# Rotary halves rearranged inside SBUF, and one buffer for each set of queries, in a two-block transformer kernel

## The chip, the cores and the metric

One core of a Trainium2 chip runs the whole program in one launch. The metric is the device time of one execution in microseconds (us), the median over several. The engines are TensorE (PE, with its weight loads PEld), VectorE (DVE), ScalarE (ACT), GpSimd (POOL) and SyncE (SP). SP and POOL also issue DMA transfers, each on a queue of its own; all transfers run on the same 16 DMA engines.

## The reference

512 tokens of 1024 features pass two blocks. Block 1 has a bidirectional chunked retention with 8 heads of 64 query/key features, a Fourier branch and a feed-forward with a convolution. Block 2 has gated spatial mixing, windowed attention with 16 query heads and 4 key heads of 64 features, and a feed-forward of 16 experts, each of which takes the 64 tokens that fit it best. All of it is in float32. What matters here is that queries and keys are turned by position before they are used:

```
def rope_2d(t, row, col):
    ...
    half = RET_QK_DIM // 2
    t1, t2 = t[..., :half], t[..., half:]
    return jnp.concatenate([t1 * cos - t2 * sin, t1 * sin + t2 * cos], axis=-1).astype(t.dtype)

q = rope_2d(split_heads(q, RET_HEADS), row, col) * q_scale
k = rope_2d(split_heads(k, RET_HEADS), row, col)
...
s_loc = jnp.einsum('bqkrd,bskd->bkrqs', qn, kn, preferred_element_type=jnp.float32) * scale
```

## The kernel before, in words

Activations lie transposed, with features on the 128 partitions and the 512 tokens along the row. A dense layer (`dense_T`, L226) computes 128 output features at a time, a chunk: 8 steps over the 1024 input features, and at each step three products (`mm3`, L221), because every float32 operand is split into a high and a low part that TensorE multiplies at full rate. So a chunk is 24 products with 512 columns. `dense_tok` (L241) is the same with tokens on the output's partitions. The weights come by SP (`w_dma_to`, L98), are split by ScalarE and VectorE (`w_split_to`, L113) three tiles ahead, and are used in the order of one list. Every engine works through its instructions in the order in which the program writes them; where one waits, all behind it on that engine wait.

The weights' columns are sorted so that one chunk holds the first rotary halves of four heads (32 features each) and the next chunk their second halves. VectorE turns them: `rope_pair` (L790) in block 1 and `rope_pair2` (L1228) in block 2 take the two chunks t1, t2 from PSUM and write a tile `rr` with two parts, r1 and r2. In it partition 32 h + i holds feature i of head h. The score products need both halves of a head one under the other on 64 partitions. That rearrangement is the subject. Before, `packer` (L393) does it by way of DRAM: two stores on POOL, one for each half, and fetches on POOL that read the tile back in the other order:

```
d = dram.tile([4, 2, 32, n], dt, name=name)
...
eng.dma_start(d[:, b], src[:, b])
...
eng.dma_start(dst, d.rearrange("h b p t -> (b p) h t"))
```

Where both partition halves need the same data, the fetch is done twice (to partitions 0 to 63 and 64 to 127). The places are:
- block 1, two batches of four heads (loop over `bt`, L805): queries into `qd`, keys into `kd`, then the projection of the values (`dense_tok("v", ...)`, L879), then `scores` (L831), which begins with transposes of `kd` (L837).
- the context's keys of block 2 (`epi_ck`, L1106): `kct` into `kcd`, split at L1140.
- the keys of block 2 (`epi_k2`, L1275): into `kdd`, split into `kH`, `kL` at L1430.
- the queries of block 2 (`epi_q2`, L1255), four sets of four heads, each two chunks: ScalarE and VectorE split `rr` into `rh` and `rl` (`split`, L107), which are stored by four transfers. The high part is fetched to partitions 0 to 63 and the low part to 64 to 127 of `qS`, which has two buffers: sets 0 and 1 at once (`q_fetch`, L1249), sets 2 and 3 in the fourth unit of the attention (L1452), when the first two are no longer read. `rr`, `rh` and `rl` have one buffer each.

After the queries follow two half chunks of a gate (`gb_half`, L1299) and the values `v2`, then eight units of attention (`unit`, L1317): per head four products into two banks of PSUM (L1334 to L1337), two operations of VectorE into `pt` (L1338, L1341) and an exponential on ScalarE. At the end of the program come the experts: 384 tiles of weights of 1 MB each, issued on SP (`x_dma_to`, L1487), the first while the attention's output is projected.

Of the kernel before, what the change touches and what calls it, by code (L numbers as in the profile page):

```python
# [42 lines left out]
def block_kernel(ctx: ExitStack, tc: tile.TileContext, A, out):  # L43
# [106 lines left out]
    def ring(stay=None):  # L150
        """a pair of buffers for activations, RINGB in turn; four of them outlive the dense layers."""
        if stay is None:
            stay = turns[0] % RINGB >= RINGB - 4
            turns[0] += 1
        pool, n = (rpool, 4) if stay else (wpool, RINGB - 4)
        return tuple(pool.tile([128, L], F32R, name=t, tag=t, bufs=n) for t in ("aH", "aL"))

# [68 lines left out]
    def dense_T(keys, acts, epi, n=L, kc=KD, first=2, pre=None):  # L226
        """out^T chunk j = W_j^T h^T, weights stationary; the first chunks share the pass over k."""
# [13 lines left out]
    def dense_tok(key, g, acts, ntok, cols, ntiles, epi, mid=None):  # L241
        """out[token, cols] = h W, activations stationary."""
# [19 lines left out]
    # modulation vectors that are needed later: products and sums along rows of the transposed  # L262
    # weights on VectorE, a part with every tile of weights
# [59 lines left out]
    def rsqrt_(v, nt, tagp):  # L323
        """v -> 1/sqrt(v), with one Newton step."""
# [20 lines left out]
    def bcast(r, nt, p):  # L345
        """[token] per partition -> [128, tokens], the same on every partition."""
# [22 lines left out]
    def modnorm(src, pB, a, b, dst, n=L, ks=range(KD)):  # L369
        """dst[k] = split of (src(k) * rstd) * a(k) + b(k); two chunks in flight."""  # L370
# [22 lines left out]
    def packer(name, n, dt=F32):  # L393
        """rotary halves of four heads [(head, 32), half, n] -> [(half, 32), head, n] by way of DRAM."""
        d = dram.tile([4, 2, 32, n], dt, name=name)

        def store(eng, src):
            for b in range(2):
                eng.dma_start(d[:, b], src[:, b])

        def fetch(eng, dst):
            eng.dma_start(dst, d.rearrange("h b p t -> (b p) h t"))
        return store, fetch

    # =====================================================================
    # block 1
    # =====================================================================
# [37 lines left out]
    def pair_mm(kp):  # L445
        """shift and scale of two chunks of features: the partial sums."""
# [29 lines left out]
    def warm(n):  # L476
        """products nobody reads, to keep the clock of TensorE up."""
# [12 lines left out]
    def first_split(j, h, l):  # L490
        """the first weights; the context's buffers hold two of them until its norm."""
        split(h, l, raws.pop(j))
        sched["ns"] += 1
        sched["nu"] += 1
        ws[j] = (h, l)
# [40 lines left out]
    def ctx_norm(cx, cH, cL, a, b):  # L536
        """the three parts of the norm of a context, to be spread over other work."""
# [37 lines left out]
    # the first projections run along with the arrival of the modulation  # L575
# [95 lines left out]
    # context of block 1: the two retention states  # L671
    # decays: lg = -exp(a), and the decay weights of the context tokens
# [8 lines left out]
    # decays of a chunk: its last state, the states' updates by token, queries to states, keys to queries  # L681
# [21 lines left out]
    # fourier mixing  # L703
# [79 lines left out]
    # retention, two batches of four heads  # L783
# [3 lines left out]

    packs = [packer(f"pk{i}", L) for i in range(4)]
# [16 lines left out]
    for bt in range(2):  # L805
# [3 lines left out]
        def epi_qk(j, ps, qd=qd, kd=kd):  # L809
# [7 lines left out]
            def emit(rr):  # L817
                store, fetch = packs.pop()
                store(nc.gpsimd, rr)
                fetch(nc.gpsimd, dst[0:64])  # L820
                fetch(nc.gpsimd, dst[64:128])
# [9 lines left out]
        def scores(h4, qd=qd, kd=kd, bt=bt):  # L831
            """within chunks: scores of keys (on partitions) and queries; keys by token for the states."""
# [20 lines left out]
        def states(h4, ke, bt=bt):  # L853
            """the states that each chunk meets: forward on partitions 0-63, backward on 64-127."""
# [39 lines left out]
        for h4 in range(4):  # L894
            ke, P, qs = nxt
            # gate projection of the head
# [52 lines left out]
    # the gates of the retention branch, while the last heads are normalized  # L949
# [9 lines left out]
    def merge_stage(key, acts, d_g, d_m, pool, tag, bufs, free, bias=None, hook=None):  # L959
        """ring chunks of d_m + d_g * (W^T acts), both operands from DRAM."""  # L960
# [49 lines left out]
    # feed-forward with the depthwise convolution  # L1010
# [86 lines left out]
    # =====================================================================  # L1097
    # block 2
    # =====================================================================
    # k, v of the context  # L1100
# [5 lines left out]
    def epi_ck(j, ps):  # L1106
        nc.scalar.activation(kct[:, j], ps, AF.Copy)
        if j == 1:
            store, fetch = packer("pkc", 256)
            store(nc.gpsimd, kct)  # L1110
            fetch(nc.gpsimd, kcd[0:64])
            fetch(nc.gpsimd, kcd[64:128])
    dense_T([("ck2", j) for j in range(2)], chl, epi_ck, n=256)

    # final norm of block 1 and first norm of block 2 from two sums
# [31 lines left out]
    # gated spatial mixing  # L1147
# [9 lines left out]
    def spatial_bias():  # L1157
        """the sums of the spatial weights times the shift join the spatial bias."""
# [56 lines left out]
    # window attention  # L1215
# [12 lines left out]
    def rope_pair2(t1, t2, emit):  # L1228
        ab = rq.tile([128, 2, L], F32, name="ab2", tag="ab2", bufs=1)
        rr = rq.tile([128, 2, L], F32, name="rr", tag="rr", bufs=1)  # L1230
# [16 lines left out]
    qfetch = {}  # L1247

    def q_fetch(kv):  # L1249
        q = ap.tile([128, 4, L], F32R, name="qS", tag="qS", bufs=2)  # L1250
        for i, fetch in enumerate(qfetch.pop(kv)):
# [809 lines left out]
```

## Time and profile before

| what | us |
|---|---|
| median of 3 runs | 2402.28 (2400.93 to 2404.88) |
| span of the profiled execution | 2399.6 |
| PE busy | 2252.9 (94%) |
| DVE, ACT, POOL busy | 1062.8, 658.2, 148.0 |
| chain that ended last, by engine | PE 62%, DMA 32%, ACT 2%, DVE 2% |

The span runs from the first to the last instruction of one profiled execution. That execution's own device time isn't listed apart; the median of the runs is 2.7 us above the span. The profile has several views: the chain of waits (what released what, from the last instruction back), tables of busy time by stretches of the span, rows of each engine in order of time with the idle time before each and what ended it, and the DMA issues with the time from issue to landing. [...]

### The profile page before, as it was taken

How to read it: one execution, taken by the hardware profiler on the slowest of the kernel's cores; microseconds unless marked ns; L12 is line 12 of the kernel's file. 1: busy time of each engine (PE TensorE's matmuls, PEld its weight loads, DVE VectorE, ACT ScalarE, POOL GpSimd, SP SyncE). 2: the span in 40 equal slices, each digit the busy share in tenths (PEclk: the TensorE clock that was granted, in tenths of full speed). 3: DMA queues.
4: the chain of work that ended last, by engine and by line, in shares of the span. 5: the costliest groups of instructions: out<-in, count | busy, mean ns of one | idle time of the engine just before them, and what ended most of it. 6: DMA issues, size and time to landing. Idle time of an engine off the chain costs nothing.

```text
span 2399.6 us, 28202 instructions
## 1 busy us (share of the span) xinstructions
PE 2252.9 (94%) x11052; PEld 1452.8 (61%) x11052; DVE 1062.8 (44%) x2059; ACT 658.2 (27%) x1033; POOL 148.0 (6%) x248
## 2 busy tenths in 40 slices
PE   9998999999999999998899999999898989898987
PEld 6887878878888887887776784434232323232322
DVE  4644666679787865435467552112111111111112
ACT  5532234344243544321366431000000000000002
POOL 0211000100112110001111000000000000000000
PEclk9999999999999999999899999999999999999999
DMA  8646254734456553246521488999999999999996
GB/s 311 237 169 193 82 157 156 258 117 153 157 186 212 159 153 106 88 128 157 148 67 27 153 322 349 410 420 420 420 421 420 420 421 420 420 421 420 420 421 277
DMA packets 138869, 623.68 MB, mean 260 GB/s; under 512 B 23600, under 2 KB 28336, under 8 KB 89712
## 3 DMA queue, kind: packets, MB, share of 16 engines
q1 hardware_dynamic: 109200, 557.59, 60.0%
q0 software_dynamic: 29536, 64.28, 9.8%
q8 instruction: 87, 1.43, 0.2%
q14 instruction: 46, 0.38, 0.0%
HBM read 600.01 MB, written 21.76 MB: 259 GB/s over the span
## 4 chain that ended last, share of the span: by engine, by line
PE 62%; DMA 32%; ACT 2%; DVE 2%; issue 1%; POOL 0%; SPq 0%; DVEq 0%; POOLq 0%; ACTq 0%
DMA xw<-in_w_exp_dram 27%; PE mm L222 12%; PE mm L224 12%; PE mm L223 12%; PE pgu L1760 5%; PE py L1818 3%; DMA pk<-rr 2%; DMA pq<-rl 2%; PE sm L1383 1%; PE mm L1371 1%; PE b L255 1%; PE b L253 1%; PE b L254 1%; PE b L222 1%; PE ps L1693 1%
## 5 line engine op out<-in xcount | busy, mean ns | idle before, releaser
L1760 PE MATMUL pgu<-xw,xt 128*64 128x512 f32 x2032 | 481.1, 602 | 56.8 <-DMA xw<-in_w_exp_dram 52.6
L222 PE MATMUL mm<-aH,wh 128*128 128x512 f32 (+1 forms) x1104 | 422.8, 383 | 6.7 <-DVE ab L1234 3.4
L224 PE MATMUL mm<-aH,wl 128*128 128x512 f32 (+1 forms) x1104 | 420.3, 381 | 3.8 <-DVE wl L131 3.8
L223 PE MATMUL mm<-aL,wh 128*128 128x512 f32 (+1 forms) x1104 | 420.0, 380 | 0.0
L1760 PEld LDWEIGHTS pgu<-xw,xt 128*64 128x64 f32 x2032 | 131.3, 136 | 355.3 <-issue 196.8
L131 DVE TENSOR_TENSOR wl<-wraw,wh 128x1024 fp32r<-128x1024 f32 (+1 forms) x212 | 256.2, 1213 | 172.2 <-ACT wh L122 171.8
L122 ACT ACTIVATE wh<-wraw 128x1024 fp32r<-128x1024 f32 (+1 forms) x212 | 220.0, 1044 | 253.2 <-PE mm L223 182.7
L222 PEld LDWEIGHTS mm<-aH,wh 128*128 128x128 f32 x1104 | 210.2, 190 | 46.7 <-issue 2.9
L224 PEld LDWEIGHTS mm<-aH,wl 128*128 128x128 f32 x1104 | 210.0, 190 | 43.6 <-DVE wl L131 4.8
L1818 PE MATMUL py<-xw,hTe 128*64 128x512 f32 x944 | 215.0, 598 | 19.4 <-DMA xw<-in_w_exp_dram 19.3
L223 PEld LDWEIGHTS mm<-aL,wh 128*128 128x128 f32 x1104 | 210.0, 190 | 38.0 <-DVE aL L383 0.4
L1818 PEld LDWEIGHTS py<-xw,hTe 128*64 128x64 f32 x944 | 64.9, 136 | 158.0 <-issue 111.4
L1788 DVE TENSOR_TENSOR eg<-pgu,eg 128x512 f32<-128x512 f32 x32 | 22.1, 692 | 253.8 <-PE pgu L1760 244.6
L1831 DVE SCALAR_TENSOR_TENSOR y<-py,sw,g2B 128x512 f32<-128x512 f32 x15 | 11.3, 751 | 221.1 <-PE py L1818 221.1
L1750 ACT ACTIVATE hTe<-pT 128x512 f32<-128x512 f32 x32 | 19.1, 597 | 313.6 <-PE pT L1749 313.6
L1726 DVE TENSOR_TENSOR aH<-ps,aH 128x512 f32<-128x512 f32 x56 | 38.8, 692 | 123.2 <-PE ps L1723 123.2
L108 ACT ACTIVATE yh<-y 128x512 fp32r<-128x512 f32 x17 | 10.7, 630 | 254.7 <-DVE y L1831 239.8
L282 POOL DMA_DIRECT2D mraw<-in_w_adaT_dram x96 | 51.5, 537 | 304.1 <-DVE mod L297 298.4
L1873 POOL TENSOR_TENSOR aH<-aH,fg 128x512 f32<-128x512 f32 x4 | 5.0, 1279 | 1037.1 <-ACT sqf L1872 1037.1
L222 PE MATMUL mm<-gH,wh 128*128 128x512 f32 x176 | 68.6, 390 | 0.0
L224 PE MATMUL mm<-gH,wl 128*128 128x512 f32 x176 | 68.6, 390 | 0.0
L223 PE MATMUL mm<-gL,wh 128*128 128x512 f32 x176 | 68.5, 389 | 0.0
(488 smaller groups left out, 3108.1 us busy)
## 6 DMA issues: line engine op xcount, KB each, us to landing
xw<-in_w_exp_dram SPq DMA_DIRECT2D x379, 1024.0 KB, 19.9
mraw<-in_w_adaT_dram POOLq DMA_DIRECT2D x96, 256.0 KB, 2.9
wraw<-in_w_up_dram SPq DMA_DIRECT2D x44, 512.0 KB, 3.8
wraw<-in_w_kv_tok_dram SPq DMA_DIRECT2D x20, 512.0 KB, 4.3
wraw<-in_w_bg_dram SPq DMA_DIRECT2D x16, 512.0 KB, 3.7
mraw<-in_w_modT_dram POOLq DMA_DIRECT2D x32, 256.0 KB, 4.6
mraw<-in_w_modT_dram SPq DMA_DIRECT2D x32, 256.0 KB, 4.2
wraw<-in_w_out_dram SPq DMA_DIRECT2D x16, 512.0 KB, 4.9
```

Of the source, the lines that this page charges most:

```text
L122: nc.scalar.activation(h[:, :sz], r[:, :sz], AF.Copy)
L131: nc.vector.tensor_tensor(*lows.pop(0), OP.subtract)
L222: nc.tensor.matmul(ps, wh, xh, start=first, stop=False)
L223: nc.tensor.matmul(ps, wh, xl, start=False, stop=False)
L224: nc.tensor.matmul(ps, wl, xh, start=False, stop=last)
L253: nc.tensor.matmul(ps[t][:, :cols], xh[:, ts], wh[:, s], start=k == 0, stop=False)
L254: nc.tensor.matmul(ps[t][:, :cols], xl[:, ts], wh[:, s], start=False, stop=False)
L255: nc.tensor.matmul(ps[t][:, :cols], xh[:, ts], wl[:, s], start=False, stop=k == KD - 1)
L282: eng.dma_start(t, A["w_modT" if b == 1 else "w_adaT"][c, hf])
L1726: nc.vector.tensor_tensor(x, p, x if e else xtok[:, t, c], OP.add)
L1760: nc.tensor.matmul(pgu[w][64 * i:64 * i + 64, :], xt[:, kq, es], t[2 * k + i], start=kq == 0, stop=kq == 7, skip_group_check=True)
L1818: nc.tensor.matmul(py[64 * hf:64 * hf + 64, :], lhs, t[2 * i + hf], start=f8 == 0 and i == 0, stop=f8 == 7 and i == 1, skip_group_check=True)
```

## The change

`packer` goes, and so do its tiles in DRAM. `pack` moves each of the eight pieces of 32 partitions (head h, half b) from its place in SBUF to its new place with a transfer of its own on POOL; `pack_twice` then copies partitions 0 to 63 to 64 to 127 with one more. The queries of block 2 are packed at once into four buffers of `qS`, and the late fetches fall away. `rr`, `rh` and `rl` of block 2 have two buffers. The reserve in SBUF for POOL's DMA descriptors is set to 2048 bytes of each partition. Comments and doc strings are taken out, which moves line numbers; they aren't shown here.

```
-    def packer(name, n, dt=F32):
-        d = dram.tile([4, 2, 32, n], dt, name=name)
-
-        def store(eng, src):
+    def pack(eng, dst, src, base=0):
+        for h in range(4):
             for b in range(2):
-                eng.dma_start(d[:, b], src[:, b])
-
-        def fetch(eng, dst):
-            eng.dma_start(dst, d.rearrange("h b p t -> (b p) h t"))
-        return store, fetch
+                eng.dma_start(dst[base + 32 * b:base + 32 * b + 32, h], src[32 * h:32 * h + 32, b])
+
+    def pack_twice(eng, dst, src):
+        pack(eng, dst, src)
+        eng.dma_start(dst[64:128], dst[0:64])
...
-    packs = [packer(f"pk{i}", L) for i in range(4)]
...
             def emit(rr):
-                store, fetch = packs.pop()
-                store(nc.gpsimd, rr)
-                fetch(nc.gpsimd, dst[0:64])
-                fetch(nc.gpsimd, dst[64:128])
+                pack_twice(nc.gpsimd, dst, rr)
...
-            store, fetch = packer("pkc", 256)
-            store(nc.gpsimd, kct)
-            fetch(nc.gpsimd, kcd[0:64])
-            fetch(nc.gpsimd, kcd[64:128])
+            pack_twice(nc.gpsimd, kcd, kct)
...
-        rr = rq.tile([128, 2, L], F32, name="rr", tag="rr", bufs=1)
+        rr = rq.tile([128, 2, L], F32, name="rr", tag="rr", bufs=2)
...
-    qfetch = {}
-
-    def q_fetch(kv):
-        q = ap.tile([128, 4, L], F32R, name="qS", tag="qS", bufs=2)
-        for i, fetch in enumerate(qfetch.pop(kv)):
-            fetch(nc.gpsimd, q[i * 64:i * 64 + 64])
-        qS[kv] = q
...
             def emit(rr):
-                rh = rq.tile([128, 2, L], F32R, name="rh", tag="rh", bufs=1)
-                rl = rq.tile([128, 2, L], F32R, name="rl", tag="rl", bufs=1)
+                rh = rq.tile([128, 2, L], F32R, name="rh", tag="rh", bufs=2)
+                rl = rq.tile([128, 2, L], F32R, name="rl", tag="rl", bufs=2)
                 split(rh, rl, rr)
-                qfetch[kv] = []
-                for i, s in enumerate((rh, rl)):
-                    store, fetch = packer(f"pq{kv}{i}", L, F32R)
-                    store(nc.gpsimd, s)
-                    qfetch[kv].append(fetch)
-                if kv < 2:
-                    q_fetch(kv)
+                qS[kv] = ap.tile([128, 4, L], F32R, name="qS", tag="qS", bufs=4)
+                pack(nc.gpsimd, qS[kv], rh)
+                pack(nc.gpsimd, qS[kv], rl, 64)
...
-            store, fetch = packer("pk2", L)
-            store(nc.gpsimd, rr)
-            fetch(nc.gpsimd, kdd[0:64])
-            fetch(nc.gpsimd, kdd[64:128])
+            pack_twice(nc.gpsimd, kdd, rr)
...
-            if u == 3 and ia in (3, 7):
-                q_fetch(2 + ia // 4)
...
-    nc = _bacc.Bacc("TRN2", target_bir_lowering=False, num_devices=1)
+    nc = _bacc.Bacc("TRN2", target_bir_lowering=False, num_devices=1, dynamic_dma_scratch_size=2048)
```

The instructions on POOL in block 1, both batches, before (`pk` are the tiles in DRAM):

```order
L399 DMA pk_1520<-rr 4x32x512 x2
L402 DMA qd<-pk_1520 64x4x512 x2
L399 DMA pk_1519<-rr 4x32x512 x2
L402 DMA kd<-pk_1519 64x4x512 x2
L399 DMA pk_1518<-rr 4x32x512 x2
L402 DMA qd<-pk_1518 64x4x512 x2
L399 DMA pk_1517<-rr 4x32x512 x2
L402 DMA kd<-pk_1517 64x4x512 x2
```

And now:

```order
L397 DMA qd<-rr 32x512 x8
L401 DMA qd<-qd 64x2048
L397 DMA kd<-rr 32x512 x8
L401 DMA kd<-kd 64x2048
L397 DMA qd<-rr 32x512 x8
L401 DMA qd<-qd 64x2048
L397 DMA kd<-rr 32x512 x8
L401 DMA kd<-kd 64x2048
```

Four transfers of each pack have become nine, in the same place of POOL's order; the ninth reads what the eight before wrote.

POOL again, in block 2 at the first set of queries, with the semaphores that each instruction waits for. DMASW0 to DMASW7 are the eight that POOL's transfers take in turn. Before:

```order
L399 DMA pq_8478<-rh 4x32x512 [waits Activation_49]
L399 DMA pq_8478<-rh 4x32x512
L399 DMA pq_8481<-rl 4x32x512 [waits DVE_49]
L399 DMA pq_8481<-rl 4x32x512
L402 DMA qS<-pq_8478 64x4x512 [waits DMASW7_49,DMASW6_49]
L402 DMA qS<-pq_8481 64x4x512 [waits DMASW1_49,DMASW0_49]
L399 DMA pq_8561<-rh 4x32x512 [waits DMASW4_49,Activation_49]
```

And now, the first set from its last piece of `rh` on:

```order
L397 DMA qS<-rh 32x512 [waits DMASW3_49]
L397 DMA qS<-rl 32x512 [waits DMASW4_49,DVE_49]
L397 DMA qS<-rl 32x512 [waits DMASW5_49]
L397 DMA qS<-rl 32x512 [waits DMASW6_49]
L397 DMA qS<-rl 32x512 [waits DMASW7_49]
L397 DMA qS<-rl 32x512 [waits DMASW0_49]
L397 DMA qS<-rl 32x512 [waits DMASW1_49]
```

The fetches' waits for the stores of the same set are gone; each piece waits for the transfer that used its semaphore last, eight transfers before.

ScalarE in the queries of block 2, at the second and third set (`rh` is the queries' high part, `wh` that of the weights). Before:

```order
L108 ACTIVATE rh<-rr 128x1024 [waits DMASW6_49,DMASW7_49,DVE_49,Activation_49]
L108 ACTIVATE kH<-kdd 128x2048 [waits DMASW5_49,DMASW4_49]
L122 ACTIVATE wh<-wraw 128x1024 [waits DMAHW6_49,PE_49]
L122 ACTIVATE wh<-wraw 128x1024 [waits DMAHW7_49,PE_49,Activation_49]
L108 ACTIVATE rh<-rr 128x1024 [waits DMASW4_49,DMASW5_49,DVE_49,Activation_49]
```

And now:

```order
L108 ACTIVATE rh<-rr 128x1024 [waits DVE_49]
L108 ACTIVATE kH<-kdd 128x2048 [waits DMASW4_49,DMASW5_49,DMASW3_49,DMASW6_49,DMASW2_49,DMASW7_49,DMASW1_49,DMASW0_49]
L122 ACTIVATE wh<-wraw 128x1024 [waits DMAHW6_49,PE_49,Activation_49]
L122 ACTIVATE wh<-wraw 128x1024 [waits DMAHW7_49,PE_49,Activation_49]
L108 ACTIVATE rh<-rr 128x1024 [waits DMASW4_49,DMASW3_49,DMASW5_49,DMASW2_49,DMASW6_49,DMASW1_49,DMASW7_49,DMASW0_49,DVE_49]
```

The order is the same. The second `rh` waits for no transfer any more; the third waits for the pieces of the first set, where it had waited for the stores of the second.

## Rows read from the trace of the kernel before

**Rows 1.** The chain of waits: start, duration (us), and what it is.

```profile
213.45 14.51 DMA pk<-rr
...
1148.79 14.73 DMA pq<-rl
...
1676.55 19.83 DMA xw<-in_w_exp_dram
```

**Rows 2.** TensorE in order of time: start, duration, instruction, idle before, its releaser.

```profile
236.22 1.09 PE L837 MATMUL mm<-ident,kd 128*128 128x128 f32 x4 [8.43 <-issue]
...
329.57 0.63 PE L837 MATMUL mm<-ident,kd 128*128 128x128 f32 x4 [4.37 <-DMA kd<-pk]
...
1081.72 0.39 PE L222 MATMUL mm<-aH,wh 128*128 128x512 f32 x1
...
1134.05 0.79 PE L224 MATMUL mm<-aH,wl 128*128 128x512 f32 x1 [2.55 <-DVE wl L131]
...
1173.37 0.28 PE L1334 MATMUL b<-kcH,qS 128*128 128x256 f32 x1
...
1184.87 0.58 PE L1334 MATMUL b<-kcH,qS 128*128 128x256 f32 x1 [3.67 <-DVE mx L1338]
```

**Rows 3.** Stretches: length, busy time (and count) by engine, PEclk, DMA share, GB/s.

```profile
core 0: us, PE busy (x) PEld busy (x) DVE busy (x) ACT busy (x) POOL busy (x), PEclk, DMA share, GB/s
1170.00:1173.36 3.36, 3.36 (x30) 3.36 (x29) 0.00 (x0) 0.87 (x3) 0.00 (x0) 1.00 0.99 276
1081.70:1103.60 21.90, 21.90 (x98) 18.14 (x97) 10.02 (x14) 4.13 (x4) 2.00 (x3) 1.00 0.49 153
236.20:241.60 5.40, 5.38 (x18) 4.37 (x19) 2.95 (x6) 0.00 (x0) 0.00 (x0) 0.51 0.02 3
329.60:337.10 7.50, 7.50 (x24) 6.05 (x25) 3.79 (x6) 1.65 (x3) 0.00 (x0) 0.54 0.24 66
1173.40:1190.50 17.10, 13.43 (x91) 12.97 (x90) 6.79 (x26) 9.04 (x19) 0.00 (x0) 0.80 0.31 106
```

**Rows 4.** POOL and VectorE in block 1, in order of time.

```profile
200.87 0.72 POOL L399 DMA_DIRECT2D pk<-rr  x1 [0.98 <-DVE rr L799]
...
208.84 0.69 DVE L799 TENSOR_TENSOR rr<-P 128x512 f32<-128x512 f32 x1
...
228.50 1.27 POOL L402 DMA_DIRECT2D kd<-pk  x2 [14.34 <-DMA pk<-rr]
...
297.15 0.71 POOL L399 DMA_DIRECT2D pk<-rr  x1 [1.33 <-DVE gv L915]
```

**Rows 5.** VectorE and ScalarE in block 2, in order of time.

```profile
1118.91 0.69 DVE L1232 TENSOR_TENSOR ab<-mm,rope 128x512 f32<-128x512 f32 x1 [0.95 <-PE mm L224]
...
1121.68 0.69 DVE L1236 TENSOR_TENSOR rr<-ab 128x512 f32<-128x512 f32 x1
...
1161.14 1.06 ACT L108 ACTIVATE rh<-rr 128x1024 fp32r<-128x1024 f32 x1 [14.12 <-DMA pq<-rh]
...
1178.19 0.48 DVE L1338 CUSTOM_DVE_ANT_0 pt<-b,amask,nsink 128x256 f32<-128x256 f32 x1 [9.92 <-PE mm L224]
```

**Rows 6.** Groups of POOL by line: count, busy us, mean ns, idle before, releasers.

```profile
L399 POOL DMA_DIRECT2D pk<-rr x10 | 7.2, 723 | 95.3 <-DVE rr L796 78.7 <-DVE rr L1233 13.3 <-DVE gv L915 1.3
L402 POOL DMA_DIRECT2D qS<-pq x8 | 5.1, 643 | 48.9 <-PE b L1337 24.4 <-DMA pq<-rh 20.0 <-DMA pq<-rl 4.6
L1211 POOL DMA_DIRECT2D ma_d<-gat x8 | 4.3, 542 | 166.6 <-DVE gat L1210 166.6
```

**Rows 7.** DMA issues: count, KB each, median us from issue to landing.

```profile
kdd<-pk POOLq DMA_DIRECT2D x2, 512.0 KB, 6.6
ma_d<-gat POOLq DMA_DIRECT2D x8, 256.0 KB, 2.3
pq<-rl POOLq DMA_DIRECT2D x8, 256.0 KB, 13.1
```

**Rows 8.** SyncE's queue: a wait (total, times, longest), and an issue in time.

```profile
SPq L1473 <- DVE aL L1413: 40.9, 1, 40.9
...
1369.32 0.43 SPq L1507 DMA_DIRECT2D xw<-in_w_exp_dram  x1
```

## The prediction

> **What bounds the kernel now.** The views were read from coarse to fine. The chain of waits [rows 1] comes first: in its last third it is made of expert-weight loads, one after the other at 19.8 us per megabyte tile, so there the end is set by when that stream starts. Earlier it is TensorE's products, broken by transfers of the rotary halves: one of 14.5 us in block 1, one of 14.7 us in block 2. The reader is to see that the round trips through DRAM lie on the chain and are not hidden.
>
> TensorE's own rows [rows 2] show where it stood still for them: 8.43 us and 4.37 us before the first score products of the two batches of block 1; in block 2 the queries' stretch has its largest stall of 2.55 us, and 3.67 us follow in the first attention unit. [...]
>
> Why the stalls are there: the rows of POOL in block 1 [rows 4] show the query stores issued at 200.87 us and the key fetch only at 228.50, because POOL, in order, waits for the landing of each store before it can issue the fetch, and the key stores stand behind the query fetch. In block 2 [rows 5] ScalarE waits 14.12 us to write `rh`, because its only buffer is still being stored; the splits of the weights stand behind it on ScalarE and VectorE, and TensorE waits for those. The first score operation of VectorE then stands 9.92 us more: its buffer lies where `rl` was, and the last `rl` store (issued 1165) is still on its way. The row names TensorE, whose products (L1334 at 1173.37) were long done, so I read it as the store.
>
> **The recoverable time.** Block 1: 8.43 + 4.37 us of standing [rows 2]; 5.40 x (1 - 0.51) = 2.65 and 7.50 x (1 - 0.54) = 3.45 us of half clock [rows 3]. Sum 18.9 us.
> Block 2: from the first product of `k2` (1081.72) to the first of unit 0 (1173.37) 91.65 us pass [rows 2]. At full clock a 512-column product takes 21.90/96 = 0.228 us and a 256-column one 3.36/28 = 0.120 us [rows 3] (two products at the edges of each stretch are not counted). The stretch has 10 chunks of 24 of the former (54.7 us) and 48 + 96 of the latter (17.3 us): 72.0 us. So 19.6 us are lost; then 3.67 us of standing, and (1 - 0.80) x 2 x 17.1 = 6.8 us at half clock, of which some 1.3 lie in that stall: (6.8 - 1.3)/2 = 2.8 us. Sum 26.1 us. Together **45.0 us**.
>
> **What replaces it.** The change removes 28 stores and 20 fetches (2 and 2 for each of four packs in block 1, the context keys and `k2`; 4 and 2 for each of four sets of queries) and adds 112 pieces of 32 partitions (8 for each of the six, 16 for each of the four) and 6 copies between partition halves. All are issued on POOL, 118 for 48. Two unknowns decide: c, the issue time on POOL, and T, the time to landing. Neither form occurs before, so both are bounded.
> c: POOL's DMA rows [rows 6] are 0.542 us (128 rows, one dimension), 0.643 (fetch) and 0.723 (store in four groups). The new ones have a quarter of the rows of the first; I take **0.64**, the fetch, the only one on less than 128 partitions; ends 0.54 and 0.74.
> T: landings [rows 7] are 2.3 us for a 256 KB store of 128 rows, 6.6 for the fetch of 512 KB, 13.1 for the query store. I take **3 us** for 64 KB, near the first, because the slow rows are all stores whose outer dimension is 4, or fetches queued in pairs; ends 2.3 and 13.1. For the copy between halves (512 KB in one) I take 5, under the pair's 6.6.
> [...]
>
> Block 1, first batch: the first piece waits for r1, the second for r2 (200.87) [rows 4]; seven issues end at 200.87 + 7 x 0.64 = 205.4, land at 208.4, the copy is issued by 209.0. The keys' r2 is ready at 208.84 + 0.69 = 209.5 [rows 4]; seven issues to 214.0, landed 217.0, copy issued 217.7, landed 222.7. TensorE needs them when its values' products end, at 236.22 - 8.43 = 227.8 [rows 2]: 5.1 us to spare. Second batch: r2 at 297.15 [rows 4], needed at 329.57 - 4.37 = 325.2, 28.05 us against 26.9: covered too. Both stalls go, with their half clock. What is late next is nothing on TensorE: it goes straight on into the score products. If the cover is gone (T over about 5 us, which counts twice and in the copy), a stall of the excess comes back.
>
> Block 2: `rr`, `rh`, `rl` have two buffers, so ScalarE no longer waits for the previous store; behind its `rh` stand the splits of the weights that TensorE needs next. With a rope of 3.5 us from the last product (1118.91 less 0.95 idle, to 1121.68 + 0.69, the chunk's end near 1118.9 [rows 5]) plus 1.06 for `rh` [rows 5], pair i is ready 4.6 us after its chunk: pair 0 at 1081.72 + 4 x 5.47 + 4.6 = 1108.2, the others each 10.94 us later. POOL needs 16 x 0.64 = 10.2 us for a pair, less than TensorE's 10.94: it keeps up. The last pair is ready at 1141.0, issued by 1151.2, landed at 1154.2; unit 0 begins on TensorE at 1173.37 - 19.6 = 1153.8 and its first operation on VectorE some 0.6 us later, at 1154.4. Even a late one has cover: TensorE has the products of two heads and two half gates, 1.0 + 48 x 0.12 = 6.8 us, before it needs a bank back. Keeping up holds to 0.75 us for a transfer (1108.2 + 64 x 0.75 + 3 + 1.1 for the first two operations of VectorE, 0.48 us each [rows 5] and their small follow-ups, = 1160.3, against 1153.8 + 6.8 = 1160.6): above the upper end of c.
>
> At nothing I cost the context keys (9 issues for 4: their split on ScalarE stands behind the norm, not behind the transfer), the fetches in the fourth unit that fall away (TensorE was full there) and the new addresses of the two extra query buffers; POOL's rows show no new wait that is not long met.
>
> Does the gain reach the end? SyncE's queue waits 40.9 us for the last attention output, and the first expert tile is issued at 1369.32 [rows 8], behind it in order. So the stream of rows 1 starts earlier by what attention gains, and all of it is passed on.
>
> **The sum.** 45.0 us less 1 us left for small stalls: 44 us. The profiled span is 2399.6 us, the median of the runs 2402.28, 2.7 above; 2399.6 - 44 + 2.7 = **2358 us**.
>
> **The rivals.**
> *POOL or the landings are half-slow.* With c = 0.74 and T = 6.6 us (the fetch row), block 1 keeps 233.2 - 227.8 = 5.4 and 4.3 us of stalls with their half clock, so it saves 3 of its 18.9 us; in block 2 POOL's DMAs turn in eight semaphores, each waiting for the one eight before (the order rows), so the period is 6.6/8 = 0.83 us, and 1108.2 + 64 x 0.83 + 6.6 + 1.1 - 1160.6 = 8.5 us of stall and some 2.8 of half clock remain: 14.8 saved. Sum 18 us: 2384. For it speaks that the DMA engines were busy in these stretches (a share of 0.99 at 1170 [rows 3]); against it, that much of this load is the round trips themselves.
> *Slower: POOL becomes the bound.* Place: the 64 pieces of the queries, and `rl`'s landing that unit 0 waits for. With the 13.1 us of the query store as T [rows 7] the period is 13.1/8 = 1.64 us: block 2 loses 1108.2 + 105 + 14.2 - 1160.6 = 67 us and 3 of clock, block 1 some 39: 109 instead of 45, so 2466. It decides from a period of about 1.2 us, where 64 x 1.2 - 48.2 = 29 us there, with its clock, and 13 in block 1 eat the 45. A smaller reserve for POOL's descriptors, which the change also makes, would act in the same place; no row shows a wait for it. Against all this stands that no POOL row exceeds 0.74 us [rows 6].
> [...] Back-to-back rows of POOL at 0.64 us show that issue overlaps, so I give it little.
> *No effect.* The stream of expert weights could be bound by something else, so that an earlier attention only waits longer: 2398 to 2407. Rows 8 speak against it.
>
> **How the numbers follow.** Forecast (2354 to 2362) 0.74; half-slow (2362 to 2390) 0.17; no effect 0.04; slower 0.05. The range takes the forecast and the near half of the half-slow case: 2353 to 2378. Faster 0.91, the same 0.04, slower 0.05, where 0.2% (4.8 us) is about what a measurement of this kernel can tell from no change.
>
> **What would show it.** Right: TensorE without the stalls before L837's line and in the queries' stretch, clock 1.0 there; small POOL rows of 0.5 to 0.7 us landing in 2 to 4 us; unit 0 starting some 38 us earlier; the first expert tile some 44 us earlier. Wrong: POOL rows or waits of a lane that add up to over 0.75 us per piece, or a first expert tile that moves and an end that doesn't.

## The result, and the profile after

The changed kernel takes 2363.79 us (median of 4 runs, 2362.11 to 2366.85) against 2402.73 us of the kernel before in the same comparison: 38.9 us less, a ratio of 0.9837 with a 95% interval of 0.9822 to 0.9851 (36 to 43 us). The span of its profiled execution is 2360.3 us, of the kernel before 2399.6.

TensorE of the changed kernel in order of time (start, duration, instruction, idle before and its releaser), at the places of [rows 2]:

```profile
226.85 0.63 PE L830 MATMUL mm<-ident,kd 128*128 128x128 f32 x4
...
313.61 0.66 PE L830 MATMUL mm<-ident,kd 128*128 128x128 f32 x4 [0.19 <-DMA kd<-kd]
...
1063.38 0.39 PE L222 MATMUL mm<-aH,wh 128*128 128x512 f32 x1
...
1135.05 0.28 PE L1309 MATMUL b<-kcH,qS 128*128 128x256 f32 x1
...
1148.12 0.58 PE L1309 MATMUL b<-kcH,qS 128*128 128x256 f32 x1 [3.94 <-DVE mx L1313]
```

The stalls of 8.43 and 4.37 us in block 1 are gone, but the second leaves 0.19 us, released by the copy `kd<-kd`: the keys come just in time. Between the first product of `k2` and unit 0 there is no stall left. In unit 0 there is one, of 3.94 us where 3.67 stood before.

The stretches that answer to [rows 3], with PEclk, the granted TensorE clock as a share of full speed, and the DMA share:

```profile
core 0: us, PE busy (x) PEld busy (x) DVE busy (x) ACT busy (x) POOL busy (x), PEclk, DMA share, GB/s
226.80:232.20 5.40, 5.40 (x29) 4.47 (x29) 3.79 (x6) 3.48 (x6) 0.00 (x0) 1.00 0.15 49
313.60:321.10 7.50, 7.49 (x38) 5.90 (x40) 4.85 (x8) 5.29 (x9) 0.00 (x0) 1.00 0.33 114
1135.00:1152.10 17.10, 12.82 (x85) 11.64 (x85) 6.70 (x25) 7.59 (x17) 1.90 (x4) 0.90 0.33 81
```

Of these three stretches the clock stays at 1.00 in the two of block 1 and falls in that of unit 0: 0.90 over 17.1 us costs (1 - 0.90) x 17.1 = 1.7 us, beside the 3.94 us. Right behind the stall, from 1148.00 to 1150.00 us, it is 0.52.

POOL in order of time, block 1's first batch and the first set of queries (answering to [rows 4]):

```profile
200.08 3.43 POOL L397 DMA_DIRECT2D qd<-rr  x7 [0.90 <-DVE rr L795]
209.09 0.52 POOL L401 DMA_DIRECT2D qd<-qd  x1 [5.58 <-DMA qd<-rr]
209.60 3.43 POOL L397 DMA_DIRECT2D kd<-rr  x7
...
221.17 0.52 POOL L401 DMA_DIRECT2D kd<-kd  x1 [7.12 <-DMA kd<-rr]
...
1090.25 3.43 POOL L397 DMA_DIRECT2D qS<-rh  x7
...
1096.33 0.49 POOL L397 DMA_DIRECT2D qS<-rl  x1 [0.83 <-DMA qS<-rh]
1097.48 0.49 POOL L397 DMA_DIRECT2D qS<-rl  x1 [0.66 <-DMA qS<-rh]
...
1139.09 0.49 POOL L397 DMA_DIRECT2D qS<-rl  x1 [2.67 <-DMA qS<-rh]
```

A piece costs 0.49 us on POOL. But inside a set POOL waits again and again for a piece issued earlier. From 1090.25 to 1139.09 + 0.49 the 64 pieces of the queries take 49.3 us, 0.77 us each. Some 18 us of that POOL is idle: 13 us end with the landing of an earlier piece or copy, 2.9 us with an operation of ScalarE, and for the rest the profile names no releaser.

The DMA issues (count, KB each, median us from issue to landing), answering to [rows 7]:

```profile
qS<-rh POOLq DMA_DIRECT2D x32, 64.0 KB, 5.9
qS<-rl POOLq DMA_DIRECT2D x32, 64.0 KB, 4.8
qd<-rr POOLq DMA_DIRECT2D x16, 64.0 KB, 1.9
kd<-rr POOLq DMA_DIRECT2D x16, 64.0 KB, 6.2
kd<-kd POOLq DMA_DIRECT2D x2, 512.0 KB, 6.3
```

The stall in unit 0, on VectorE and ScalarE in order of time (the first line answers to the last of [rows 5]):

```profile
1141.44 0.48 DVE L1313 CUSTOM_DVE_ANT_0 pt<-b,amask,nsink 128x256 f32<-128x256 f32 x1 [9.71 <-DMA qS<-rl]
...
1142.64 1.28 ACT L1319 ACT_TABLE_LOAD   x1 [7.01 <-DVE mx L1316]
...
1145.36 1.04 ACT L122 ACTIVATE wh<-wraw 128x1024 fp32r<-128x1024 f32 x1
...
1146.43 1.23 DVE L131 TENSOR_TENSOR wl<-wraw,wh 128x1024 fp32r<-128x1024 f32 x1 [2.82 <-ACT wh L122]
1147.58 0.48 DVE L1313 CUSTOM_DVE_ANT_0 pt<-b,amask,nsink 128x256 f32<-128x256 f32 x1
```

VectorE's first score operation stands 6.4 us behind TensorE's first score product (1135.05), now with the `rl` piece named as its releaser. After two heads VectorE reaches a split of weights and waits for `wh`, which ScalarE writes only after a table load and two exponentials. The third head follows at 1147.58, and TensorE gets back the bank that it needs for its fifth head.

SyncE's queue (answering to [rows 8]): the wait, and the first expert tile, 37.75 us earlier.

```profile
SPq L1446 <- DVE aL L1388: 40.8, 1, 40.8
...
1331.57 0.43 SPq L1480 DMA_DIRECT2D xw<-in_w_exp_dram  x1
```

Three marks divide each kernel's time: the first product of `k2`, the first product of unit 0 and the first expert tile. From these rows of TensorE and SyncE, one profiled execution each:

| kernel | `k2` starts | `k2` to unit 0 | unit 0 to first tile | first tile | median |
|---|---|---|---|---|---|
| before | 1081.72 | 91.65 | 195.95 | 1369.32 | 2402.73 |
| changed | 1063.38 | 71.67 | 196.52 | 1331.57 | 2363.79 |
| e1 block 1 alone | 1063.28 | 83.77 | 199.98 | 1347.03 | 2377.40 |
| e2 buffers alone | 1079.16 | 71.67 | 201.13 | 1351.96 | 2386.94 |
| e3 one buffer | 1063.52 | 78.42 | 192.34 | 1334.28 | 2367.27 |
| e4 `pt` apart | 1063.03 | 71.67 | 190.55 | 1325.25 | 2358.08 |
| e5 other store | 1062.63 | 71.67 | 190.49 | 1324.79 | 2357.03 |
| e6 DRAM in block 2 | 1065.18 | 71.67 | 190.79 | 1327.64 | 2360.06 |
| e7 e5, apart | 1064.09 | 71.67 | 190.49 | 1326.25 | 2357.60 |
| e8 reserve alone | 1084.24 | 86.11 | 199.47 | 1369.83 | 2401.38 |
| e9 four groups | 1082.15 | 92.35 | 198.71 | 1373.21 | 2403.35 |
| e10 eight groups | 1084.27 | 75.65 | 195.00 | 1354.93 | 2387.69 |
| e11 changed again | 1063.45 | 71.67 | 195.29 | 1330.42 | 2362.49 |
| e12 one store | 1065.64 | 71.67 | 190.45 | 1327.77 | 2357.88 |

Eight of these executions agree on 71.67 us for the second stretch, so that is its length without a loss; for the third it is 190.5. The kernel before lost 20.0 and 5.5 us there. The change got back 18.3 us before `k2` and all 20.0 us of the second stretch, and it still loses 6.0 us in the third. 18.34 + 19.98 - 0.57 = 37.75 us at the first tile. From there to the end the two kernels take 1030.2 and 1028.8 us, so the expert part only moves.

### The profile page after: what moved, and what is told of

Same layout as the page of the kernel before. It is cut to its first block, busy times and chain, and to the rows that moved or that the text cites. A ratio compares the mean times of both kernels' runs of the same rounds, so it can differ in the third digit from the quotient of the medians.

```text
span 2360.3 us, 28316 instructions
## 1 busy us (share of the span) xinstructions
PE 2237.4 (95%) x11052; PEld 1441.4 (61%) x11052; DVE 1062.8 (45%) x2059; ACT 658.0 (28%) x1033; POOL 173.5 (7%) x318
## 4 chain that ended last, share of the span: by engine, by line
PE 53%; DMA 30%; ACT 2%; DVE 2%; issue 1%; POOL 0%; SPq 0%; DVEq 0%; ACTq 0%; POOLq 0%
DMA xw<-in_w_exp_dram 27%; PE mm L224 10%; PE mm L222 10%; PE mm L223 10%; PE pgu L1733 6%; PE py L1791 3%; PE sm L1358 1%; PE mm L1346 1%; PE ps L1666 1%; PE pT L1666 1%; PE py L1819 1%; DMA qS<-rh 1%; PE b L1309 1%; PE b L255 1%; PE b L253 1%
## 5 line engine op out<-in xcount | busy, mean ns | idle before, releaser
L222 PEld LDWEIGHTS mm<-aH,wh 128*128 128x128 f32 x1104 | 208.5, 189 | 40.8 <-ACT aH L380 2.6
L1760 ACT ACTIVATE eg<-pgu 128x512 f32<-128x512 f32 x32 | 19.1, 597 | 177.8 <-PE pgu L1733 177.8
```

Of the source, the lines that this page charges most:

```text
L222: nc.tensor.matmul(ps, wh, xh, start=first, stop=False)
```

## Experiments

### Block 1 alone, and buffers alone

e1 is the kernel before with `pack_twice` in `epi_qk` alone. e2 is the kernel before with this alone:

```
-        rr = rq.tile([128, 2, L], F32, name="rr", tag="rr", bufs=1)
+        rr = rq.tile([128, 2, L], F32, name="rr", tag="rr", bufs=2)
...
-                rh = rq.tile([128, 2, L], F32R, name="rh", tag="rh", bufs=1)
-                rl = rq.tile([128, 2, L], F32R, name="rl", tag="rl", bufs=1)
+                rh = rq.tile([128, 2, L], F32R, name="rh", tag="rh", bufs=2)
+                rl = rq.tile([128, 2, L], F32R, name="rl", tag="rl", bufs=2)
```

> The kernel before, with the pieces and the copy in block 1 alone; everything in block 2 by way of DRAM as before. My account says that block 1 and block 2 are separate terms: the stalls of 8.43 and 4.37 us before the score products and their half clock go (18.9 us counted, some 0.3 us kept, since in the changed kernel the second copy came 0.19 us late), and from there to the end all is as before, 18 to 19 us earlier: 2402.7 - 18.5 = 2384 us, unit 0 of the attention at about 1155. Rival: the weights and the context's transfers that block 1's pieces push aside come back as stalls in block 2, or the transfers of block 2 take more of the same waits; then unit 0 starts later than 1157 and the time is 2388 to 2395 us.

> The kernel before, by way of DRAM throughout, with two buffers for rr, rh and rl of block 2 and nothing else changed. Theory that the buffers free ScalarE and with it the splits of the weights: the stalls between 1109 and 1173 shrink from 19.6 to 3 to 6 us with their half clock; the last rl store still lands some 13 us after its issue, so a stall of 5 to 9 us stands in the first attention unit; together 10 to 16 us faster, 2387 to 2393 us. Theory that only the shorter transfer frees them (the sets follow each other on POOL, which waits 10 us per round trip): at most 4 us faster, 2399 to 2403 us. Block 1 keeps its 18.9 us of loss by either.

e1: 2377.4 us, ratio 0.9897 (0.9881 to 0.9912), 26.2 us less than the 2403.61 of before beside it, instead of 18.5: outside what either account had given. Block 1 gave what was counted: `k2` starts 18.4 us earlier. But block 2, unchanged, lost 12.1 + 9.5 us instead of 20.0 + 5.5. So block 2's loss is not a fixed number. e8, with the old transfers throughout, lost 14.4 + 9.0. Why the long round trips fall now this way, now that way, one profile each doesn't tell.

e2: 2386.9 us, ratio 0.9934 (0.9919 to 0.9950). ScalarE in order of time:

```profile
1115.50 1.06 ACT L108 ACTIVATE rh<-rr 128x1024 fp32r<-128x1024 f32 x1 [7.92 <-DVE rr L1236]
1126.98 1.06 ACT L108 ACTIVATE rh<-rr 128x1024 fp32r<-128x1024 f32 x1 [6.70 <-DVE rr L1236]
1137.26 1.06 ACT L108 ACTIVATE rh<-rr 128x1024 fp32r<-128x1024 f32 x1 [6.46 <-DVE rr L1236]
```

and VectorE's first score operation:

```profile
1160.81 0.48 DVE L1338 CUSTOM_DVE_ANT_0 pt<-b,amask,nsink 128x256 f32<-128x256 f32 x1 [13.30 <-DMA pq<-rl]
```

With the DRAM trip as slow as ever (`rh` 11.5, `rl` 10.5 us to landing) `rh` waits for VectorE alone, and `k2` to unit 0 takes 71.67 us. The second buffers suffice for that stretch. The price comes in the next one: unit 0 waits for the late `rl` store and 10.6 us are lost there.

### One buffer with the pieces

e3 is the changed kernel with the three `bufs=2` of the block above set back to 1.

> The changed kernel with one buffer each for rr, rh and rl of block 2. Theory that the transfer's form carries most: a set's pieces take 16 x 0.77 = 12.3 us on POOL in any case, and the next rh can be written while the eight of rl are on their way, so the single buffers add some 1 to 2 us per set and a stall of a weight's split or two: 2366 to 2372 us. Theory that the second buffers are what gives block 2 its gain: ScalarE and VectorE stand 5 us or more for each of three sets, TensorE follows with its clock, 15 to 20 us come back, 2379 to 2384 us.

2367.3 us, ratio 0.9851 (0.9836 to 0.9866), 3.5 us above the changed kernel, where the two intervals overlap, and inside the first theory's range. The second stretch loses 6.75 us (stalls of 0.65 and 2.48 us for a split of weights; behind the second, products of 512 columns follow each other after 0.43 us, where it is 0.23 before); unit 0 begins later and so waits less. Pieces alone get back 13.2 of the 20.0 us, buffers alone all of it: two remedies of one loss, which mustn't be added.

### The score tiles apart from `rl`

e4 is the changed kernel; `rh` and `rl` get a pool at the other end of SBUF, and the score tiles two pools, of which the first is opened before that of `rh` and `rl` is closed and the second only at the second unit:

```
-    rqs, rq, rope = rope_open()
+    rhs = ExitStack(); rhl = rhs.enter_context(tc.tile_pool(name="rhl", bufs=1)); rqs, rq, rope = rope_open()
...
-    pp = at.enter_context(tc.tile_pool(name="pp", bufs=1, side="right"))
+    pps = [at.enter_context(tc.tile_pool(name="pp0", bufs=1, side="right"))]; rhs.close()
...
+        if u == 1: pps.append(at.enter_context(tc.tile_pool(name="pp1", bufs=1, side="right")))
```

> The changed kernel, in which the score tiles of the first attention unit no longer lie where rh and rl lie (these two have a pool of their own, which the second unit's tiles take over). Theory that the stall of 3.94 us in unit 0 and its half clock (3.4 us at half) come from the landing of the last rl piece: VectorE starts within 1 us of the first score products (about 1135.5 instead of 1141.44), the stall and the half clock go, 5.6 us faster than the changed kernel, 2358 us. Rival: the stall is that of ScalarE's table load and exponentials, with the split of a weight behind them and VectorE behind that, whenever VectorE starts; then it moves up with VectorE and some 2 to 4 us of stall stay: 2361 to 2364 us.

2358.1 us, ratio 0.9815 (0.9801 to 0.9828). VectorE's first score operation, in order of time:

```profile
1135.13 0.48 DVE L1313 CUSTOM_DVE_ANT_0 pt<-b,amask,nsink 128x256 f32<-128x256 f32 x1 [3.74 <-PE b L1310]
```

It follows TensorE's product by 0.4 us, although the last `rl` piece lands 4.9 us after that product; the stall and its half clock are gone (PEclk 1.00 from 1134.70 to 1151.80 us), and the first tile is issued 6.3 us earlier. ScalarE's table load is still there (1136.34, 1.28 us), so the rival falls: the chain behind it costs TensorE nothing when it starts on time.

### Another form of store, still by way of DRAM

e5 is the kernel before with another layout of its tile in DRAM, and nothing else:

```
-        d = dram.tile([4, 2, 32, n], dt, name=name)
+        d = dram.tile([2, 128, n], dt, name=name)
...
-                eng.dma_start(d[:, b], src[:, b])
+                eng.dma_start(d[b], src[:, b])
...
-            eng.dma_start(dst, d.rearrange("h b p t -> (b p) h t"))
+            for b in range(2): eng.dma_start(dst[32 * b:32 * b + 32], d[b].rearrange("(h p) t -> p h t", p=32))
```

e9 has the fetches of e5 but stores in four groups again (`[2, 4, 33, n]`, a row of gap behind each group); e10 has eight groups (`[2, 8, 17, n]`) with fetches of 16 partitions.

> The kernel before, still by way of DRAM, but with its tile in DRAM laid out as half, 128 partitions, tokens: each store is 128 rows instead of 4 groups of 32, and each fetch becomes two of 32 partitions. Theory that the form of the store made the round trip long (13.1 us with an outer dimension of 4 against 2.3 us for 128 rows): the stores land in 2.5 to 5 us, POOL waits 3 us for them instead of 10 to 14, both stalls before the score products of block 1 go and most of those in block 2's queries, at most a small stall in unit 0 stays: 2362 to 2372 us, all or nearly all that the change gave, without a transfer inside SBUF. Rival, that the trip through DRAM as such, two transfers one after the other behind a landing, costs the time: stores land in 8 us or more or the fetches take it up, the stall of 8.43 us shrinks to 3 or more and block 2 keeps over half of its losses: 2380 to 2395 us.

> e5 with one thing put back: the rows of the DRAM tile lie in 4 groups of 32 with a gap of a row between them, so that each store again has an outer dimension of 4; the fetches are those of e5 (two of 32 partitions). It parts the form of the store from the form of the fetch. Theory that the store alone makes the difference: stores land in 8 to 13 us as in the kernel before, the stalls of 8 and 4 us in block 1 and those of block 2 are back, 2390 to 2405 us. Rival, that e5 gained by its fetches (two that overlap where one was waited for): stores land in under 6 us or their landing does not matter, at most 2 us of stall in block 1, 2357 to 2372 us.

> As e9, but in 8 groups of 16 rows, the fetches in four of 16 partitions. [...] Worked out from the rows: the stores' median landings are 10 us with 4 groups and 3 us with 128 rows; of that some 2 us are fixed, so 8 us of transfer become 4, a landing of 5 to 7 us; the stalls of block 1 shrink to 0 to 3 us and block 2 keeps a part: 2360 to 2380 us. Rival, that any store in groups is slow, whatever their number: landings of 8 to 13 us and 2390 to 2405 us. Rival, that 8 are enough: landings under 4 us and 2356 to 2360 us.

e5: 2357.0 us, ratio 0.9804 (0.9785 to 0.9824), quicker than I had put down for either theory. e9: 2403.4 us, ratio 0.9989 (0.9970 to 1.0008). e10: 2387.7 us, ratio 0.9936 (0.9919 to 0.9954).

The DMA issues of e5, then of e9, then of e10:

```profile
pk<-rr POOLq DMA_DIRECT2D x10, 256.0 KB, 3.1
pq<-rh POOLq DMA_DIRECT2D x8, 256.0 KB, 3.1
```

```profile
pk<-rr POOLq DMA_DIRECT2D x10, 256.0 KB, 10.2
pq<-rh POOLq DMA_DIRECT2D x8, 256.0 KB, 10.1
```

```profile
pk<-rr POOLq DMA_DIRECT2D x10, 256.0 KB, 5.0
pq<-rh POOLq DMA_DIRECT2D x8, 256.0 KB, 6.1
```

The same 256 KB of `rr` land in 10.2, 5.0 and 3.1 us with 4, 8 and 128 as the outer dimension; the `rl` stores, which stand behind those of `rh`, in 13.9, 9.9 and 4.7 us. From 198 to 204 us, in which each kernel's first two stores were under way, POOL's queue moved 0.12 MB in e9, 0.47 in e10 and 0.52 in e5, against 0.20 in the kernel before; in e10 and e5 the first query fetches were issued by then too. In the kernel before 4 packets of that queue were under way at a time from 201.0 to 203.5 us, while the first store was alone. That some 2 us of a landing are fixed and that eight groups halve the rest was my estimate; no run shows a fixed part, and the whole median went from 10.2 to 5.0 us.

POOL and TensorE in block 1 of e5:

```profile
200.11 0.54 POOL L399 DMA_DIRECT2D pk<-rr  x1 [1.19 <-DVE rr L799]
202.35 2.26 POOL L402 DMA_DIRECT2D qd<-pk  x4 [1.70 <-DMA pk<-rr]
...
214.99 2.21 POOL L402 DMA_DIRECT2D kd<-pk  x4 [5.37 <-DMA pk<-rr]
```

```profile
226.87 0.60 PE L837 MATMUL mm<-ident,kd 128*128 128x128 f32 x4
```

and of e9:

```profile
213.46 1.40 POOL L399 DMA_DIRECT2D pk<-rr  x2
224.82 0.57 POOL L402 DMA_DIRECT2D kd<-pk  x1 [9.95 <-DMA pk<-rr]
```

```profile
234.91 1.09 PE L837 MATMUL mm<-ident,kd 128*128 128x128 f32 x4 [6.51 <-DMA kd<-pk]
```

e5 has no transfer inside SBUF, one buffer for `rr`, `rh` and `rl`, two query buffers and the late fetches. It has none of the stalls, not even that of unit 0: its last `rl` store lands before unit 0 begins. e9 differs from it in the store's groups alone and has all of them back. So the whole loss hung on the form of the store.

e10's time lies outside what I expected, although the `rr` stores land as expected by the median. Block 2 recovers in part (4.0 + 4.5 us lost). In block 1 the stalls stay at 8.08 and 5.47 us: the key fetches wait 8.51 us for their stores, which were issued right behind eight query fetches (9.2 us to landing, where e5's four took 6.1), and are then eight themselves. Those key stores took 10.3 and 10.5 us in the first batch, e5's 7.7 and 6.2. As e10 changes the stores and the fetches at once, how much of block 1's loss is due to either is not shown.

### DRAM in block 2 with buffers, and everything at once

e6 is e1 with the second buffers of e2 and the pools of e4; e7 is e5 with the same two.

> Block 1 with pieces as in e1, block 2 by way of DRAM with stores in four groups and two query buffers as before, but with two buffers for rr, rh and rl and the first unit's score tiles apart from them as in e4. It differs from e4 in the transport of block 2 alone (and in the two late fetches). Theory that in block 2 it is not the transport that costs but what waits for its buffers: no stall over 1 us from the first product of k2 to the second attention unit, first tile of experts within 2 us of e4 (1325.25), 2356 to 2361 us. Rival, that the long stores still hold something (the splits behind rh, the fetch of the second set, the second unit's tiles, the late fetches in the fourth unit): 5 us or more of stalls with their clock stay, 2364 to 2372 us.

> e5 with two buffers for rr, rh and rl and the first unit's score tiles apart from them: everything by way of DRAM with the other form of store, no transfer inside SBUF. If the store's form and the buffers are all there is, no stall stays before the score products of block 1 or in block 2, 2355 to 2361 us as e4. If the trip through DRAM is too long for block 1's keys (two stores, four fetches, twice, within 27 us from the queries' r2), a stall of 1 to 6 us with its clock stays before the first score products of each batch: 2362 to 2375 us.

e6: 2360.1 us, ratio 0.9825 (0.9803 to 0.9847), with stores that still take 10.8 and 10.4 us to land. Its second and third stretch are 71.67 and 190.79 us. Its first tile is 2.4 us behind e4's: 2.15 us were lost before `k2`, 1.35 of them in a late key copy in block 1, and 0.2 after it. Its last `rl` store lands 2.7 us after unit 0 begins, and nothing stands for it. So in block 2 the slow trip itself costs nothing once nothing waits for its buffers. e7: 2357.6 us, ratio 0.9807 (0.9790 to 0.9824), as e5: buffers add nothing where the stores are quick (medians of 2.9 to 4.3 us to landing).

### The reserve alone

e8 is the kernel before with `dynamic_dma_scratch_size=2048`.

> The kernel before with the smaller reserve for POOL's descriptors (2048 bytes) and nothing else. Theory that the reserve is not used up by this kernel's transfers: all stalls and POOL's issue times as before, 2400 to 2406 us. Rival, that a smaller reserve makes POOL wait before an issue: its rows grow from 0.72 us or show idle time without a releaser, the round trips get longer, 2408 us or more. The run also tells how far the stalls of block 2 repeat in a second build.

2401.4 us, ratio 0.9993 (0.9981 to 1.0005). Its stores cost 727 ns on POOL for 723 before: the reserve does nothing here, with 48 transfers; for all 118 of the changed kernel it was not varied.

### The changed kernel beside a shorter one

e11 is the changed kernel again; e12 is e5 with `d` as `[128, 2, n]` and one store of 512 KB per tile (it has 14 transfers fewer than e5; the 24 in the text below is a miscount).

> The changed kernel itself, timed beside e12 on one chip. Expected as measured first, 2362 to 2366 us; the landing of the last rl piece again some 6 us after the first score products, and a stall of 3.5 to 4.2 us in unit 0.

> e5 with one store per tile: 128 rows that hold both halves, 512 KB in one transfer, so 24 transfers fewer than e5 on POOL. Theory that the landing of 128-row stores is what counts and the number of transfers not: no stall in block 1 or block 2, the first expert tile at 1324 to 1327, 2355 to 2360 us, and 4 to 8 us less than e11 on the same chip. Rival: the store can only begin when both halves are turned, 1.7 us later than the first of two, and takes the longer for its size (landing 4 to 8 us instead of 3), so that the keys of block 1, which had under 2 us to spare, come late: a stall of 1 to 4 us before the score products of each batch with its clock, 2361 to 2370 us.

On one chip e11 takes 2362.5 us (2361.0 to 2363.8) and e12 2357.9 us (2356.4 to 2359.2); the two ranges don't meet. Ratios to before: 0.9836 (0.9816 to 0.9856) and 0.9816 (0.9796 to 0.9836). e11's stall in unit 0 was 2.73 us this time, less than I had put down; VectorE and TensorE there:

```profile
1139.02 0.48 DVE L1313 CUSTOM_DVE_ANT_0 pt<-b,amask,nsink 128x256 f32<-128x256 f32 x1 [7.21 <-DMA qS<-rl]
...
1145.70 0.58 PE L1309 MATMUL b<-kcH,qS 128*128 128x256 f32 x1 [2.73 <-DVE mx L1313]
```

e12 had a stall of 1.86 us before the first score products of block 1 and none later. e12 beat the changed kernel side by side; e4, e5 and e7 have ratios as low as e12's or lower (0.9804 to 0.9815), each from a comparison of its own, with intervals that overlap a little with the changed kernel's. e5 is the smallest edit of the kernel before.

## Why the prediction was right, and where it was off

- **What bounds the kernel, and the recoverable time.** Right. Block 1 was put at 18.9 us, and `k2` starts 18.3 us earlier. The stretch from `k2` to unit 0 was put at 72.0 us without loss; it is 71.67. The products counted there took what was put down: in the changed kernel those of 512 columns on split operands follow each other after 0.23 us (1063.38 to 1063.60), where the unsplit ones of `qd` and `kd` take 0.14 us for 128 columns (eight from 227.41 to 228.50), both at a clock of 1.00. Behind the stalls of the kernel before the granted clock was 0.50 from 236.20 to 238.90, from 333.00 to 336.60 and from 1185.00 to 1188.00 us. The 45.0 us in all are what e5 recovers at the first tile: 1369.32 - 1324.79 = 44.5 us.
- **That all of it is passed on.** Right: SyncE's wait is 40.8 us again and the first tile moves by what attention gains. The rival of no effect falls.
- **c, the issue time.** Taken as 0.64 with ends 0.54 and 0.74; it is 0.49, below the lower end. The row of fetches was the wrong neighbour; the 128-row store (0.542) was nearer.
- **T, the landing.** Mis-sized: 3 us taken, measured 1.9 for the queries of block 1, but 5.9 and 4.8 for those of block 2, 6.2 for block 1's keys and 6.3 for their copy (medians). The queries' pieces were not held by c but mostly by the turn of the eight semaphores, as the first rival said: 0.77 us each where 0.83 stood there. The time, 2363.8 us, also lies in that rival's bracket (2362 to 2390), which had a chance of 0.17, and not in the forecast's (2354 to 2362); the range held because it took in the nearer half of the rival's. The last was to be issued by 1151.2 on the clock of before, 1132.9 on that of the changed kernel (18.3 less); it was issued by 1139.6. The 5.1 us to spare in block 1 were 0.4 in the first batch (the copy issued at 221.17 landed after 5.2 us, the score products began at 226.85) and 0.19 too few in the second. That the stalls went all the same is partly luck: the prediction's own sign for their return, T over about 5 us, was there for the keys, and c below its lower end gave some of that back. With the same pieces e11 stood 0.55 us in the second batch and e6 1.35 us in the first. The low end of T was right only for pieces with little before them: the queries of the second batch landed in 1.8 to 1.9 us.
- **"Even a late one has cover".** This is the step that failed. It gave VectorE 6.8 us, less 1.1 for its own first head, so 5.7 us behind TensorE's first score product; the runs show 1.0 us. TensorE got its bank for the third head about as forecast, 6.94 us after that product, 0.2 later than without a loss. It stands at the fifth head, for which it needs what VectorE's third head frees. What I had left out lies between VectorE's second and third head: a split that waits for `wh`, behind ScalarE's table load and two exponentials. In all nine executions in which VectorE starts late, its third head comes 6.13 us after its first score operation, and TensorE's fifth head 0.54 us later. Some of them, in us after TensorE's first score product:

  | kernel | VectorE's first score operation | TensorE's fifth head | its delay | stall before it |
  |---|---|---|---|---|
  | e5 | 0.43 | 7.71 | none | none |
  | e3 | 2.75 | 9.43 | 1.72 | 1.59 |
  | e11 | 3.89 | 10.57 | 2.86 | 2.73 |
  | before | 4.83 | 11.50 | 3.79 | 3.67 |
  | changed | 6.40 | 13.07 | 5.36 | 3.94 |

  So each microsecond by which VectorE starts later than 1.0 us behind TensorE is one by which TensorE's fifth head is late. In e11 VectorE was done with its first head 1.7 us before TensorE needed that bank, and TensorE still stood 2.73 us. The changed kernel's delay of 5.36 us is the 3.94 us and short waits at the third and fourth head. With the clock, 6.0 us are lost in the third stretch against the 1 us left for small stalls: 44 forecast, 38.9 measured. e4 shows it by taking away the wait at the start of that chain.
- **The slower rival** fell: the period of a piece was 0.77 us, far from 1.2. The pieces, of 64 KB each, overlapped: their median landings were 5.9 and 4.8 us, and all 64 took 49.3 us. e12, with 54 transfers on POOL for the same data, was quicker than the changed kernel with its 118 by 4.6 us; but e4, with all 118, took 2358.1 us, so nothing here shows that their number cost time.
- **What I saw but didn't follow.** The prediction says that the slow rows are all stores whose outer dimension is 4, or fetches queued in pairs, and then prices only the way out that the change takes. The 13.1 us of the query store were also those of `rl` stores behind the two of `rh`; in the same place with 128 rows they are 4.7. e5 and e9 show that the form of the store was at fault and not the trip through DRAM.

## What to carry to other kernels

When a round trip is slow, first compare its landing with another transfer of the same size in the same trace, and if the form differs, change the form before the route: a change of layout in three lines of a helper did here what pieces, buffers and a new pool did. Two remedies of one wait don't add up; test each alone. And where an engine that works in order seems to have cover, list what stands behind the late instruction on it, up to the next thing that another engine needs from it: here a chain of 6.1 us behind VectorE's first operation left 1.0 us of the 5.7 counted.

## What the runs showed that I had not expected

Pieces of one size landed in very different times: those of 64 KB took 1.9 us (median) for block 1's queries and 6.2 for its keys, right behind a copy of 512 KB. No run takes a neighbour in the queue away, so what made the difference stays open. To issue a store of the same 256 KB took POOL 0.72 us with 4 groups, 0.63 with 8 and 0.54 with 128 rows, less the more of them there are. And the loss of one and the same slow round trip moved between 12.1 + 9.5 and 20.7 + 8.2 us over e1, e8, e9 and the kernel before, which stays unexplained.
